# Transposing the decayed keys of a gated linear attention with VectorE and DMA in place of TensorE, with the state product one group later

## Chip, cores and metric

The kernel runs on one core of a Trainium2 chip, as one launch. The metric is the device time of that launch in microseconds (us); lower is better. All data are float32. A product that needs full precision is made of three matmuls of split operands (high x high, low x high, high x low).

## What is computed

The reference is one layer of a hybrid encoder, for 2048 positions of width 1024. One projection of x feeds two groups of heads: group A, a gated linear attention that runs over the positions in both directions, and group B, a latent attention with softmax. Their outputs go through one output projection, then a residual and a layer norm. The change lies in the backward direction of group A. Cut to that, for each head (dk 64, dv 128):

```
q_dec  = qc * exp(b)            # b: running sum of the log decay in a chunk
k_dec  = kc * exp(-b)
k_tail = kc * exp(b_last - b)
attn   = where(mask, q_dec . k_dec, 0)
o_intra = attn . vc
# from chunk to chunk:
o     = q_dec . state
state = state * exp(b_last) + k_tail^T . vc
```

The kernel works in 16 chunks of 128 positions.

## The kernel before, in words

**Stages.** `sweep_a` (L625) takes the chunks from 15 down to 0, one step for each. Then come `late_gates` (L1095), which trace the gate products of chunks 15 and 14 and load the weights of group B, and `sweep_c` (L1119), which runs over the chunks upwards. Attention and the output projection follow.

**A step of the first sweep** (step i, chunk c = 15 - i) has four groups of TensorE products over eight slices of the width: `products` with g = 0, 1, 2 (tile `ipa`, L425 to L427) and, as group 3, `gate_products` (tile `ipg`, L885), each with eight times three matmuls. Group 0 gives q and the low-rank decay input lr, group 1 gives k and a part of v, group 2 the rest of v, group 3 the gate. What hangs on them for this chunk and the chunk before is put between the matmuls. These pieces are:

- `lrT` (L929): transpose of lr on TensorE, then `z` (the log decay) and its running sums with scans on VectorE, E1 = exp(b), E2 = exp(-b) on ScalarE;
- `qx`, `kx` (L821, L834): q and k are turned by a VectorE transpose in 32x32 blocks, written with four DMAs to DRAM (`qx_s`, `kx_s`) so that the blocks land in their transposed places, and read back by `turned` (L829) with two loads each;
- `q`, `k` (L991, L1005): the decayed `qd` and `kd`, with the key dimension on the partitions;
- `kt` (L1018): four TensorE transposes of `kd`, one per head, so that the positions stand on the partitions, evicted to SBUF by ScalarE (`hi`, L371);
- `intra` (L1029): the products `Ap`, copied and masked into `At`;
- `av` (L1043): `Op` = At . V, evicted by ScalarE to `oi` and stored to DRAM (`oi_s`);
- `state` (L1054): `Up` = kt^T . V, scaled on VectorE into `Us` and stored (`su_s`); GpSimd forms `Sm` and the running state `Sb` (L1072 to L1091).

**What sets the order.** For the steps 4 to 15 the table `STEPS_A` names what follows matmul k of group g, as `(g, k)`; "prev" is the chunk of the step before, "cur" the chunk of the step. `in_order` (L387) then pins the order of the traced instructions on every engine. Steps 0 to 3 follow a list written out by hand (`ORDER_A`). What follows step 15 in the sweep (the last chunk's `q`, `k`, gate products, `kt`, `intra`, `state`, `av`) is traced in L760 to L772. What stands after the sweep and isn't pinned, such as the `memset` that clears the forward state `Sf` (L1138) or the weight splits of `late_gates` (`wmh` on ScalarE, `wml` on VectorE, both L371/L377), is placed by the scheduler that builds the program.

**Queues.** Nearly all DMAs of the sweep are issued on SyncE (SP) and its queue is in order; for chunks 1 and 0 the stores go on GpSimd's queue (`store`, L921). SP also issues the loads of x: `xaf` for the steps' own products, `xbf` (at L491) for the late gates in step 15, `xcf` for `sweep_c`, and the weights `wmr`, `wzr`.

**Buffers.** The tiles of the sweep that hold one chunk (`t512`, L926) come from the pool `g1`, most with a single buffer; its space is used by `sweep_c`'s tiles later.

Of the kernel before, what the change touches and what calls it, by code (L numbers as in the profile page):

```python
# [9 lines left out]
F32 = mybir.dt.float32  # L10
# [8 lines left out]
P = 128  # L19
# [3 lines left out]
NCH = S // P  # L23
H = 4
# [33 lines left out]
av.2 av.2 gs.3 cw.3 gs.3  # L58
"""

STEPS_A = {(0, 3): [("k", "prev")], (1, 2): [("ld", "next")], (1, 4): [("kt", "prev"), ("lrT", "cur")],
           (1, 7): [("z", "cur", 5), ("intra", "prev"), ("z", "cur", 4)], (2, 3): [("state", "prev")],
           (2, 7): [("z", "cur"), ("cw", "cur")], (3, 2): [("q", "cur")], (3, 3): [("av", "prev")]}
STEPS_A_FIRST = {**STEPS_A, (0, 3): [("q", "prev"), ("k", "prev")]}
STEPS_A_LAST = {**STEPS_A, (1, 2): [], (1, 6): [("z", "cur", 5)], (1, 7): [("intra", "prev"), ("z", "cur", 4)]}
ENGINES = tuple(getattr(mybir.EngineType, n) for n in ("PE", "Activation", "DVE", "Pool", "SP"))
LATE_ORDER = ENGINES[1], ENGINES[3], ENGINES[4]
# [293 lines left out]
class K:  # L361
# [145 lines left out]
    def run(self):  # L507
        tc, nc, ins = self.tc, self.nc, self.ins
        with ExitStack() as top:
            cp = top.enter_context(tc.tile_pool(name="const", bufs=1))  # L510
            self.cp = cp
            dp = top.enter_context(tc.tile_pool(name="scr", bufs=1, space=DRAM))
            self.qd_s = [dp.tile([P, H * P], F32, name=f"qd_s{c}") for c in range(NCH)]
            self.oi_s = [dp.tile([P, H * P], F32, name=f"oi_s{c}") for c in range(NCH)]
            self.su_s = [dp.tile([P, H * P], F32, name=f"su_s{c}") for c in range(NCH)]
            self.u_s = [dp.tile([P, H * P], F32, name=f"u_s{c}") for c in range(NCH)]
            self.qa_s = [[dp.tile([P, H, QB], F32, name=f"q{p}_s{b}") for p in "hl"] for b in range(NQB)]
            self.qr_s = [[dp.tile([H, 64, QB], F32, name=f"r{p}_s{b}") for p in "hl"] for b in range(NQB)]
            self.gm_s = [dp.tile([P, H, QB], F32, name=f"gm_s{b}") for b in range(NQB)]
            self.oa_s = [dp.tile([P, H, P], F32, name=f"oa_s{c}") for c in range(NCH)]  # L520
            self.qk_s = [[dp.tile([64, H, P], F32, name=f"{n}_s{c}") for c in range(NCH)] for n in ("qx", "kx")]
            self.r_s = [dp.tile([1, H, QB], F32, name=f"r_s{b}") for b in range(NQB)]
            self.ob_s = [dp.tile([P, H, QB], F32, name=f"ob_s{b}") for b in range(NQB)]

            ident = cp.tile([P, P], F32, name="ident")
            self.ident = ident
            self.gkv_c = cp.tile([P, 1], F32, name="gkv_c")
            self.gn_c = cp.tile([P, 1], F32, name="gn_c")
            self.cw = cp.tile([P, NCH, 3, H], F32, name="cw")

            psum = ExitStack()
            pspool = lambda n: psum.enter_context(tc.tile_pool(name=n, bufs=2, space=PSUM, reuse_waits="tile"))
            self.gp, self.ip, self.tr = pspool("gp"), pspool("ip"), pspool("tr")
            self.xfp = top.enter_context(tc.tile_pool(name="xfp", bufs=2, reuse_waits="tile"))
            edge = top.enter_context(tc.tile_pool(name="edge", bufs=1, side="right"))
            edge.tile([P, 8], F32, name="edge")
            self.keep = top.enter_context(tc.tile_pool(name="keep", bufs=1, side="right", reuse_waits="tile"))
            wgs = ExitStack()
            self.wgp = wgs.enter_context(tc.tile_pool(name="wgp", bufs=2 * NK + 1, side="right", reuse_waits="tile"))
            self.xab = wgs.enter_context(tc.tile_pool(name="xab", bufs=2, side="right"))  # L540
            self.wgate = []
            self.wl = None
            self.sweep_a()
            self.wz = top.enter_context(tc.tile_pool(name="wz", bufs=2 * NK + 1, reuse_waits="tile"))
            bcs = ExitStack()
            self.wm = bcs.enter_context(tc.tile_pool(name="wm", bufs=2 * NK + 1, reuse_waits="tile"))
            self.bc = bcs.enter_context(tc.tile_pool(name="bc", bufs=1, reuse_waits="tile"))
            self.wl = bcs.enter_context(tc.tile_pool(name="wl", bufs=2, reuse_waits="tile"))
            self.late_gates()
            wgs.close()  # L550
            rp = top.enter_context(tc.tile_pool(name="res", bufs=1, side="right", reuse_waits="tile"))
            self.ckvT_h = rp.tile([P, NKT, P], F32R, name="ckvT_h")
            self.ckvT_l = rp.tile([P, NKT, P], F32R, name="ckvT_l")
            self.kr = rp.tile([P, NKT, P], F32R, name="krs")
            self.vh = rp.tile([P, NKT, P], F32R, name="vh")
            self.vl = rp.tile([P, NKT, P], F32R, name="vl")
            self.sweep_c()
            bcs.close()
            psum.close()
            self.wof = top.enter_context(tc.tile_pool(name="wof", bufs=PRE_W, side="right", reuse_waits="tile"))  # L560
            self.attention()
# [63 lines left out]
    def sweep_a(self):  # L625
        tc, nc, ins, cp = self.tc, self.nc, self.ins, self.cp
        with ExitStack() as ctx:
# [21 lines left out]
            with tc.tile_pool(name="sta", bufs=1, reuse_waits="tile") as sta:  # L649
# [5 lines left out]
                for g, (_, n) in enumerate(A_GROUPS):  # L655
                    k = 0
# [28 lines left out]
            g1 = ctx.enter_context(tc.tile_pool(name="g1", bufs=1))  # L685
# [5 lines left out]
            run = lambda n, i: [0 for _ in getattr(self, "ga_" + n)(ch[i])]  # L691
# [9 lines left out]
            def step(i, steps):  # L701

                def after(g, k):
                    for n, d, *count in steps.get((g, k), ()):
                        j = {"prev": i - 1, "cur": i, "next": i + 2}[d]
                        if n == "ld":
                            if j < NCH:
                                next(self.ga_ld(j))
                        elif count:
                            some(n, j, *count)  # L710
                        elif (n, j) in begun:
                            for _ in begun.pop((n, j)):
                                pass
                        else:
                            run(n, j)
                for g in range(3):
                    for k in self.products(ch[i], g, after):
                        pass
                    after(g, NK - 1)
                if i and ch[i]["c"] not in LATE_GATES:  # L720
                    for k in self.gate_products(ch[i]["c"], *ch[i]["x"], ip):
                        after(3, k)
                    self.gate_end(ch[i]["c"], g1)

            self.first_lr = wdone[7][0]
            step(0, {(1, 5): [("lrT", "cur")]})
            ch[1]["x"] = self.split_x(xp, xnext, NCH - 2, "xa", "dve", 2)
            run("bst", 0)
            self.wgr = [self.wgp.tile([P, 512], F32, tag="wg", name=f"wgr{k}") for k in range(NK)]
            for k, raw in enumerate(self.wgr):  # L730
# [3 lines left out]
            for t in ORDER_A.split():  # L734
                n, i = t.split(".")
# [7 lines left out]
            for i in range(4, NCH):  # L743
                c = ch[i]["c"]
                with self.in_order(last):
# [3 lines left out]
                    else:  # L749
                        self.xlate = [self.split_x(xp, self.xb, NCH - 1, "xb")]  # L750
                        self.xraw = self.load_x(NCH - 2, "xb")
                    step(i, STEPS_A_FIRST if i == 4 else STEPS_A if c else STEPS_A_LAST)
                    if c == 1:
# [3 lines left out]
                if i == 12:  # L757
                    assert next(rope, None) is None
                    self.rope_tables(hpi)
            i = NCH - 1  # L760
            run("q", i)
            run("k", i)
            run("av", i - 1)
            for k in self.gate_products(0, *ch[i]["x"], ip):
                if k == 5:
                    run("kt", i)
            self.xlate.append(self.split_x(self.xab, self.xraw, NCH - 2, "xb", "dve", 2))
# [237 lines left out]
    def ga_k(self, d):  # L1005

        nc, c = self.nc, d["c"]
        kT = d.get("kT")
        if kT is None:
            kT = d["tr"].tile([P, H, P], F32, tag="tr", name=f"kT{c}")  # L1010
            for h in range(H):
                nc.tensor.transpose(kT[:, h], d["k2"][:, h].rearrange("p a d -> p (a d)"), self.ident)
            yield
        kd = d["kd"] = self.t512(d, "kd")
        nc.vector.tensor_tensor(kd, kT, d["E2"], ALU.mult)
        yield

    def ga_kt(self, d):  # L1018
# [1044 lines left out]
```

## Time and profile before

| | |
|---|---|
| median of three runs | 1285.17 us (1284.21 to 1286.22) |
| profiled execution | 1286.1 us, of which the span is 1284.3 us |
| TensorE (PE) busy | 1259.7 us, 98% |
| VectorE (DVE) busy | 899.4 us, 70% |
| ScalarE (ACT) busy | 755.5 us, 59% |
| GpSimd (POOL) busy | 761.1 us, 59% |
| granted TensorE clock, mean | 0.998 |
| DMA moved | 155.25 MB, mean 121 GB/s |

A row of a timeline reads: start and duration in us, engine, line of the kernel, operation, out<-in by the program's names, shape, and count of like instructions that are drawn together; in brackets, the idle time of the engine just before and what ended it. PEld is TensorE's weight load, SPq the queue of DMA issues on SyncE. In the table of waits each row is an engine's instruction, what it waited for, the total, the count and the longest in us. The steady part of the first sweep lies between 80 and 310 us; the step of chunk 0 begins at 316.76 us.

### The profile page before, as it was taken

What the parts mean: (1) busy time and instruction counts of PE and PEld (TensorE: products, weight loads), DVE (VectorE), ACT (ScalarE), POOL (GpSimd) and SP (SyncE); (2) the same over time, 40 slices, a digit from 0 to 9 for tenths busy, and PEclk for the clock granted to TensorE, in tenths of its full rate; (3) what the DMA queues carried; (4) which work ended last, traced back from release to release, by engine and by line L of the source; (5) the groups of instructions that cost most, each with busy time, mean ns of one, the idle gap of its engine ahead of it and who ended that gap; (6) DMA issues with size and microseconds to landing.
All of it is one profiled execution on the core that took longest, in us unless ns stands there. A gap on an engine that the chain in (4) does not pass through costs nothing.

```text
span 1284.3 us, 19837 instructions
## 1 busy us (share of the span) xinstructions
PE 1259.7 (98%) x7050; PEld 1109.9 (86%) x7050; DVE 899.4 (70%) x1602; ACT 755.5 (59%) x1230; POOL 761.1 (59%) x476
## 2 busy tenths in 40 slices
PE   7999999999999999999999999999999999999997
PEld 7999999999889999999788888888888888887886
DVE  6635554544575555554888888888888888479997
ACT  7544343444565655555788888888888888511110
POOL 0132323222367666650498888889999999944541
PEclk9999999999999999999999999999999999999999
DMA  8223444444755666547201111111133110375752
GB/s 293 78 79 108 115 111 114 115 105 126 255 171 184 205 205 210 194 149 228 76 1 42 41 42 50 46 54 58 58 89 93 41 42 9 123 227 193 220 189 99
DMA packets 135746, 155.25 MB, mean 121 GB/s; under 512 B 43510, under 2 KB 86142, under 8 KB 135648
## 3 DMA queue, kind: packets, MB, share of 16 engines
q1 hardware_dynamic: 127584, 151.86, 38.4%
q0 software_dynamic: 672, 2.10, 0.4%
q8 instruction: 56, 0.92, 0.4%
q10 hardware_dynamic: 7392, 0.03, 0.3%
q14 instruction: 42, 0.34, 0.2%
HBM read 100.43 MB, written 53.51 MB: 120 GB/s over the span
## 4 chain that ended last, share of the span: by engine, by line
PE 82%; DMA 5%; DVE 4%; ACT 2%; issue 2%; POOL 2%; SPq 2%; DVEq 0%; POOLq 0%; ACTq 0%
PE pz L1237 6%; PE ipm L1308 5%; PE o L425 4%; PE o L426 4%; PE o L427 4%; PE pS L1569 4%; PE pS L1570 4%; PE pS L1572 4%; PE pS L1571 4%; PE pS L1573 4%; PE ipa L425 4%; PE ipa L427 4%; PE ipa L426 4%; PE ipg L427 2%; PE ipg L425 2%
## 5 line engine op out<-in xcount | busy, mean ns | idle before, releaser
L377 POOL TENSOR_TENSOR pl<-s,ph 128x1024 fp32r<-128x1024 f32 x128 | 306.4, 2411 | 57.7 <-ACT ph L371 53.8
L1591 DVE TENSOR_TENSOR rm<-pS,rm 128x512 f32<-128x512 f32 x210 | 144.8, 689 | 36.7 <-ACT s L1578 31.5
L1578 ACT ACTIVATE s<-pS 128x1024 f32<-128x1024 f32 x128 | 131.2, 1026 | 61.8 <-PE pS L1573 52.0
L1615 DVE TENSOR_TENSOR s<-s,mb 128x1024 f32<-128x1024 f32 x128 | 151.2, 1212 | 8.9 <-PE mb L1609 8.2
L371 ACT ACTIVATE ph<-s 128x1024 fp32r<-128x1024 f32 x128 | 135.1, 1057 | 16.9 <-PE o L427 16.4
L1619 ACT ACTIVATE s<-s 128x1024 f32<-128x1024 f32 x128 | 131.4, 1050 | 12.2 <-DVE s L1615 12.1
L425 PE MATMUL ipa<-wah,xah 128*128 128x384 f32 (+1 forms) x384 | 129.7, 338 | 5.5 <-ACT wah L371 5.5
L426 PE MATMUL ipa<-wal,xah 128*128 128x384 f32 (+1 forms) x384 | 124.5, 324 | 0.5 <-DVE wal L377 0.5
L427 PE MATMUL ipa<-wah,xal 128*128 128x384 f32 (+1 forms) x384 | 124.4, 324 | 0.0
L1569 PE MATMUL pS<-qh,ckvT_h 128*128 128x512 f32 x256 | 102.7, 401 | 2.0 <-ACT s L1578 1.2
L1072 POOL TENSOR_TENSOR Sb<-Sb,Us 64x512 f32<-64x512 f32 x15 | 20.9, 1394 | 136.9 <-DVE Us L1064 127.8
L425 PE MATMUL o<-ph,vh 128*128 128x512 f32 x256 | 101.0, 395 | 0.0
L1570 PE MATMUL pS<-ql,ckvT_h 128*128 128x512 f32 x256 | 100.0, 391 | 0.0
L1572 PE MATMUL pS<-rh,krs 128*128 128x512 f32 x256 | 99.9, 390 | 0.0
L1571 PE MATMUL pS<-qh,ckvT_l 128*128 128x512 f32 x256 | 99.9, 390 | 0.0
L1573 PE MATMUL pS<-rl,krs 128*128 128x512 f32 x256 | 99.8, 390 | 0.0
L427 PE MATMUL o<-ph,vl 128*128 128x512 f32 x256 | 99.7, 389 | 0.0
L426 PE MATMUL o<-pl,vh 128*128 128x512 f32 x256 | 99.6, 389 | 0.0
L1642 DVE TENSOR_TENSOR ap<-ap,s 128x512 f32<-128x512 f32 x120 | 83.1, 693 | 2.7 <-ACT s L1619 0.7
L377 POOL TENSOR_TENSOR xal<-xaf,xah 128x1024 fp32r<-128x1024 f32 x12 | 29.7, 2477 | 87.8 <-ACT xah L371 87.8
L377 POOL TENSOR_TENSOR ol<-of,oh 128x512 fp32r<-128x512 f32 x32 | 43.2, 1352 | 62.6 <-ACT oh L371 61.9
L425 PEld LDWEIGHTS ipa<-wah,xah 128*128 128x128 f32 x384 | 72.9, 190 | 7.8 <-ACT wah L371 5.5
(308 smaller groups left out, 3595.6 us busy)
## 6 DMA issues: line engine op xcount, KB each, us to landing
xcf<-xT_dram SPq DMA_DIRECT2D x16, 512.0 KB, 5.1
xr<-x_dram SPq DMA_DIRECT2D x16, 512.0 KB, 6.4
out_dram<-rr SPq DMA_DIRECT2D x32, 256.0 KB, 2.2
xaf<-xT_dram SPq DMA_DIRECT2D x14, 512.0 KB, 4.2
oib<-oi_s SPq DMA_DIRECT2D x16, 256.0 KB, 4.0
qdb<-qd_s SPq DMA_DIRECT2D x16, 256.0 KB, 4.0
SU<-su_s SPq DMA_DIRECT2D x16, 256.0 KB, 4.1
ub<-u_s SPq DMA_DIRECT2D x16, 256.0 KB, 4.2
```

The costliest lines, as they stand in the source:

```text
L371: return nc.scalar.activation(dst, src, AF.Copy).ins
L377: return e.tensor_tensor(dst, src, hi.bitcast(F32), ALU.subtract).ins
L425: mm(out, ah, bh, start=start, stop=False)
L426: mm(out, ah, bl, start=False, stop=False)
L427: mm(out, al, bh, start=False, stop=stop)
L1569: mm(ps[:, e], kh, qh, start=True, stop=False)
L1570: mm(ps[:, e], kh, ql, start=False, stop=False)
L1571: mm(ps[:, e], kl, qh, start=False, stop=False)
L1572: mm(ps[:, e], kr, rh, start=False, stop=False)
L1573: mm(ps[:, e], kr, rl, start=False, stop=True)
L1591: V.tensor_tensor(d["rm"], src[:, e], d["rm"], ALU.max)
L1615: V.tensor_tensor(s, s, d["mb"][:, None, :].to_broadcast([P, 2, QB]), ALU.subtract)
```

## The change

For the chunks of i = 4 to 14 `kt` on TensorE is replaced by two pieces:

- `kx2`: VectorE transposes `kd` in 32x32 blocks (128 x 512), and four DMAs on SP write the result to a new DRAM tensor `kt_s`, 64 KB each, in pieces of 32 elements;
- `ktl`: one DMA of 256 KB on SP reads `kt` back into SBUF.

`kx2` stands at (1, 4), where `kt` stood, behind `lrT`; `ktl` at (2, 4). `state`, which consumes `kt`, moves from (2, 3) to (3, 6), that is ahead of the last three matmuls of the gate. Step 4, which handles chunk i = 3, keeps the old places. The chunk i = 15 still uses TensorE; the state of chunk i = 14 is traced after the third group of three matmuls of the last gate product (k == 2).

In the order of instructions: TensorE has 44 transposes fewer (11 x 4), ScalarE 11 evictions fewer, VectorE 11 transposes more, SP 55 DMA issues more. On SP the stores `su_s` of `Us` and `Sm` now stand behind the loads of k and the store of `oi`; in the last step `xbf` still stands behind them. TensorE's late-gate matmuls of `xb` stand in part ahead of the last chunk's `kt`, `Ap`, `Up` and `Op` (24 of 48, where 3 stood). On VectorE the `memset` of `Sf` stands ahead of all eight `wml`, where it stood behind five. From the first `wm` weights on the rest of the order is the same. Line numbers in the changed kernel are 2 higher from L64 on, 3 from L521, 5 from L764 and 19 from L1016 on.

```diff
--- before.py
+++ after.py
@@ -58,10 +58,12 @@
 av.2 av.2 gs.3 cw.3 gs.3
 """
 
-STEPS_A = {(0, 3): [("k", "prev")], (1, 2): [("ld", "next")], (1, 4): [("kt", "prev"), ("lrT", "cur")],
-           (1, 7): [("z", "cur", 5), ("intra", "prev"), ("z", "cur", 4)], (2, 3): [("state", "prev")],
-           (2, 7): [("z", "cur"), ("cw", "cur")], (3, 2): [("q", "cur")], (3, 3): [("av", "prev")]}
-STEPS_A_FIRST = {**STEPS_A, (0, 3): [("q", "prev"), ("k", "prev")]}
+STEPS_A = {(0, 3): [("k", "prev")], (1, 2): [("ld", "next")], (1, 4): [("lrT", "cur"), ("kx2", "prev")],
+           (1, 7): [("z", "cur", 5), ("intra", "prev"), ("z", "cur", 4)], (2, 4): [("ktl", "prev")],
+           (2, 7): [("z", "cur"), ("cw", "cur")], (3, 2): [("q", "cur")], (3, 3): [("av", "prev")],
+           (3, 6): [("state", "prev")]}
+STEPS_A_FIRST = {**STEPS_A, (0, 3): [("q", "prev"), ("k", "prev")], (1, 4): [("kt", "prev"), ("lrT", "cur")],
+                 (2, 3): [("state", "prev")], (2, 4): [], (3, 6): []}
 STEPS_A_LAST = {**STEPS_A, (1, 2): [], (1, 6): [("z", "cur", 5)], (1, 7): [("intra", "prev"), ("z", "cur", 4)]}
 ENGINES = tuple(getattr(mybir.EngineType, n) for n in ("PE", "Activation", "DVE", "Pool", "SP"))
 LATE_ORDER = ENGINES[1], ENGINES[3], ENGINES[4]
@@ -519,6 +521,7 @@
             self.gm_s = [dp.tile([P, H, QB], F32, name=f"gm_s{b}") for b in range(NQB)]
             self.oa_s = [dp.tile([P, H, P], F32, name=f"oa_s{c}") for c in range(NCH)]
             self.qk_s = [[dp.tile([64, H, P], F32, name=f"{n}_s{c}") for c in range(NCH)] for n in ("qx", "kx")]
+            self.kt_s = [dp.tile([P, H, P], F32, name=f"kt_s{c}") for c in range(NCH)]
             self.r_s = [dp.tile([1, H, QB], F32, name=f"r_s{b}") for b in range(NQB)]
             self.ob_s = [dp.tile([P, H, QB], F32, name=f"ob_s{b}") for b in range(NQB)]
 
@@ -762,6 +765,8 @@
             run("k", i)
             run("av", i - 1)
             for k in self.gate_products(0, *ch[i]["x"], ip):
+                if k == 2:
+                    run("state", i - 1)
                 if k == 5:
                     run("kt", i)
             self.xlate.append(self.split_x(self.xab, self.xraw, NCH - 2, "xb", "dve", 2))
@@ -1013,6 +1018,20 @@
             yield
         kd = d["kd"] = self.t512(d, "kd")
         nc.vector.tensor_tensor(kd, kT, d["E2"], ALU.mult)
+        yield
+
+    def ga_kx2(self, d):
+
+        t = d["g1"].tile([P, H, 4, 32], F32, tag="ktx", name=f"ktx_{d['c']}")
+        self.nc.vector.transpose(t.rearrange("p h a s -> p (h a s)"), d["kd"].rearrange("p h s -> p (h s)"))
+        dst = self.kt_s[d["c"]].rearrange("(a r) h (b t) -> b r h a t", a=4, b=4)
+        for b in range(4):
+            self.nc.sync.dma_start(dst[b], t[32 * b:32 * b + 32])
+        yield
+
+    def ga_ktl(self, d):
+        d["kt"] = self.t512(d, "kt")
+        self.nc.sync.dma_start(d["kt"], self.kt_s[d["c"]])
         yield
 
     def ga_kt(self, d):
```

## Prediction

> **What bounds the kernel now.** I read the busy table first, then busy time by stretch, then PE's waits, and last the timelines of the engines at the places where PE waits.
>
> ```profile
> span 1284.3 us, 19837 instructions
> PE 1259.7 (98%) x7050; PEld 1109.9 (86%) x7050; DVE 899.4 (70%) x1602; ACT 755.5 (59%) x1230; POOL 761.1 (59%) x476
> ```
> ```profile
> 80.00:310.00 230.00, 228.87 (x1497) 215.51 (x1496) 114.83 (x207) 100.14 (x201) 64.69 (x43) 1.00 0.41 109
> 380.00:620.00 240.00, 237.54 (x1669) 225.65 (x1668) 129.80 (x440) 140.13 (x357) 140.09 (x144) 1.00 0.59 194
> ```
> ```profile
> PE kt L1023 <- DVE kd L1015: 1.6, 1, 1.6
> PE ipm L1308 <- DVE xcl L377: 1.2, 1, 1.2
> PE lrT L933 <- DVE lr L377: 1.1, 1, 1.1
> PE Op L1047 <- DVE At L1040: 0.6, 1, 0.6
> ```
>
> The columns of the stretches are us, then PE, PEld, DVE, ACT and POOL busy. In the steady part of the first sweep (80 to 310 us) PE is busy 228.87 of 230 us, and the only wait of PE there is the 1.1 us of lrT. DVE (114.83) and ACT (100.14) are half idle. So in that stretch the kernel is bound by PE, and PE work taken out comes off the time, unless a later place cannot use it. The other three waits listed lie between 338 and 357 us, where the sweep hands over to the next stage. After 380 us PE is full again (237.54 of 240), so whatever the handover yields, plus or minus, stays to the end.
>
> **What the change removes.** Eleven chunks (4 to 14) lose four PE transposes and one ACT eviction each.
>
> ```profile
> 194.34 0.34 PE L427 MATMUL ipa<-wah,xal 128*128 128x384 f32 x1
> 194.52 0.60 PE L1023 MATMUL kt<-ident,kd 128*128 128x128 f32 x4
> 194.95 0.27 PE L933 MATMUL lrT<-ident,lr 128*98 128x128 f32 x1
> 194.98 0.42 PE L425 MATMUL ipa<-wah,xah 128*128 128x384 f32 x1
> ```
> ```profile
> L1023 PE MATMUL kt<-ident,kd x44: 270/272/273, 88.9 to 301.8; 128*128 128x128 f32 x44
> L371 ACT ACTIVATE kt<-kt x11: 597/597/599, 89.6 to 302.1; 128x512 f32<-128x512 f32 x11
> ```
>
> One transpose lasts 272 ns, but they are pipelined: what PE gives up is the spacing of starts. From the first kt (194.52) to lrT (194.95) are 0.43 us for four; I take 0.44, so 11 x 0.44 = 4.8 us at most. The eviction, 0.597 us, is on an engine with over half its time free, so I count nothing for it.
>
> One of the eleven gives nothing by itself. The 1.1 us wait of lrT in the list stands right behind a kt: PE waits there for lr, and without kt it comes 0.44 earlier and waits 0.44 longer. The chunk whose transposes stand in the last step is treated below. So up to the start of the last step 9 x 0.44 = **3.96 us** are saved.
>
> **What the change adds in each step.** A DVE transpose of 128x512, four stores to DRAM and one load, all on SP's queue; the state product Up moves from the third group of products to just before the last three gate matmuls (of 24) of the step. I lay this out in the step that begins at 188.74 and is followed by the next at 209.86 (21.12 us).
>
> ```profile
> 188.74 0.29 PE L425 MATMUL ipa<-wah,xah 128*128 128x288 f32 x1
> ...
> 209.63 0.39 PE L427 MATMUL ipg<-wgh,xal 128*128 128x512 f32 x1
> 209.86 0.29 PE L425 MATMUL ipa<-wah,xah 128*128 128x288 f32 x1
> ```
> ```profile
> 196.85 0.45 DVE L824 STREAM_TRANSPOSE kx<-ipa 128x256 f32<-128x256 f32 x1 [3.81 <-PE ipa L427]
> ```
> ```profile
> 193.07 2.59 SPq L827 DMA_DIRECT2D qx_s<-qx  x4
> 195.70 0.60 SPq L491 DMA_DIRECT2D xaf<-xT_dram  x1
> 197.09 1.62 SPq L832 DMA_DIRECT2D q<-qx_s  x2
> 198.82 2.82 SPq L827 DMA_DIRECT2D kx_s<-kx  x4
> ```
> ```profile
> DMA to landing us min/median/max: 2.2/3.0/3.4
> ```
> ```profile
> oib<-oi_s SPq DMA_DIRECT2D x16, 256.0 KB, 4.0
> ```
>
> DVE: the transpose of 128x256 takes 0.45, so twice the width lies between 0.45 and 0.9; I take 0.85. DVE idles 3.81 us just after this place (the bracket of the row), which hides it; without that cover it would delay kx, which feeds only the next step. SP: qx_s and xaf end at 196.30. The four kt_s come next. A qx_s issue takes 2.59 / 4 = 0.65 for 64 partitions' worth of half as many pieces as a kt_s; nothing in the trace issues 512 pieces of 128 bytes, so a kt_s lies between 0.65 (the cost is per issue) and 1.3 (per piece). I take 0.65, because a row of the same kind of store is nearest, and keep the other end as a rival. Then kt_s runs to 198.9 and lands by 198.9 + 3.4 = 202.3 (the landing line is that of kx_s); q to 200.5, kx_s to 203.35, the load of kt issues at 203.4 and lands 4.0 later (the 256 KB row), at **207.4**. Up starts 0.44 + 3 x 0.23 + 0.92 before 209.86, at **207.8** (0.23 is the spacing of the last two rows of PE above, 0.92 that of Up below). It is in time by 0.4 us, so each step costs nothing more. SP has 3.0 us more work in a step of 21 and keeps room.
>
> **The last step.** Here one transfer is moved past something. SP's queue is in order. Before, it issues the store of Us and of Sm of the step before at 312.21 and 312.75, and the load xbf at 316.45, 0.31 ahead of the step's start (316.76). ACT splits xbf before it evicts lr, and lrT waits for lr.
>
> ```profile
> 312.21 0.49 SPq L1065 DMA_DIRECT2D su_s<-Us  x1
> ...
> 316.45 0.83 SPq L491 DMA_DIRECT2D xbf<-xT_dram  x2
> ```
> ```profile
> 321.02 1.06 ACT L371 ACTIVATE xbh<-xbf 128x1024 fp32r<-128x1024 f32 x1 [2.13 <-DMA xbf<-xT_dram]
> ```
> ```profile
> 316.76 0.29 PE L425 MATMUL ipa<-wah,xah 128*128 128x288 f32 x1
> ```
> ```profile
> 322.55 0.60 PE L1023 MATMUL kt<-ident,kd 128*128 128x128 f32 x4
> 322.98 0.27 PE L933 MATMUL lrT<-ident,lr 128*98 128x128 f32 x1
> ...
> 338.32 0.66 PE L1023 MATMUL kt<-ident,kd 128*128 128x128 f32 x4 [1.64 <-DVE kd L1015]
> ...
> 341.39 1.16 PE L1061 MATMUL Up<-V,kt 128*128 128x128 f32 x8
> 343.82 1.16 PE L1047 MATMUL Op<-V,At 128*128 128x128 f32 x8 [0.57 <-DVE At L1040]
> ```
>
> In the changed order Up ends 3 x 0.23 = 0.7 before the step's start (call it T); Us needs about 0.8 more, so the two su_s issue (0.49 and 0.5) until T + 1.2, and xbf, behind them, at about **T + 1.4** instead of T - 0.31. It lands 4.48 after its issue now (316.45 to 320.94, 0.08 before xbh starts) and lrT is ready 1.6 after that landing (xbh 1.06, two small ACT copies, the small DVE one). That gives T + 7.45. PE is there at 322.55 - 316.76 = T + 5.79, with no kt ahead of lrT any more. So PE gets a new wait of 1.66; lrT stands at T + 7.45 instead of T + 6.22, **1.23 later**. The 0.44 of the eleventh kt is in that.
>
> Further on in the last step the changed order puts 24 of the two late gates' 48 matmuls (ipg from xb) ahead of the last Op, where 3 stood: 21 x 0.23 = **4.8 later**. In exchange kt's 1.64 wait for kd is covered (Us and kd now run beside 13 of these matmuls). The 0.57 before Op stays, as no matmul is left between Up and Op. Sum for the last Op, and for oi, its eviction and its store: -3.96 + 1.23 + 4.8 - 1.64 = **+0.4**: the stores end no earlier, while PE has 21 matmuls fewer to fill the time after it.
>
> **The handover.** DVE clears Sf, whose place in SBUF is that of the sweep's tiles, and so waits for the landing of the last oi store.
>
> ```profile
> 346.11 3.49 DVE L377 TENSOR_TENSOR wml<-wmr,wmh 128x448 fp32r<-128x448 f32 x5 [1.18 <-ACT wmh L371]
> 352.53 0.48 DVE L1138 MEMSET Sf<- 64x512 f32 x1 [2.93 <-DMA oi_s<-oi]
> 352.94 2.65 DVE L377 TENSOR_TENSOR wml<-wmr,wmh 128x448 fp32r<-128x448 f32 x3
> 355.50 2.35 DVE L377 TENSOR_TENSOR xcl<-xcf,xch 128x1024 fp32r<-128x1024 f32 x2
> ```
> ```profile
> 345.90 0.57 POOL L1051 DMA_DIRECT2D oi_s<-oi  x1
> ```
> ```profile
> 356.77 0.47 PE L1308 MATMUL ipm<-wmh,xcl 128*128 128x448 f32 x1 [1.16 <-DVE xcl L377]
> ```
>
> Now five of the eight wml subtractions stand ahead of the memset, three and xcl behind it, and PE's third ipm matmul waits 1.16 for xcl: DVE is already last here. In the changed program's order on DVE the memset stands ahead of **all eight**. The five that used to fill the wait (3.49 us by the row) now queue behind it, ahead of xcl. With oi's landing 0.4 later, xcl is ready 3.5 + 0.4 = **3.9 us later**, and PE cannot use what it saved: it waits at ipm for some 9 us instead of 1.16. DVE then runs without a pause into the weights of the next product, so nothing is given back before PE is full again from 380 us on.
>
> So a gain of 3.96 us is eaten at the handover, and 3.9 us are lost on top. The profiled execution took 1286.1 us (0.9 above the median of 1285.17) and would become 1290.0; against the median, 1285.2 + 3.9 = **1289.1**.
>
> **The rivals.**
>
> *Faster: the handover does not bind.* If the memset's wait, or DVE's order, is not what ends last at ipm, PE keeps its 4.8 less the 0.44 of the step with the lr wait: 1285.2 - 4.4 = 1280.8. For it speaks that PE is the busy engine on both sides. Against it: to let PE through, xcl would have to start near 350, nine us before the 359 that this order gives, so the memset would have to run at 343.6, before the last oi store is issued (345.90). It decides only if the Sf wait disappears.
>
> *xbf is not late.* If xbf lands in 2.8 instead of 4.48 (kx_s lands in 2.2 to 3.4 in the row above), the new 1.66 wait at lrT vanishes and only 3.9 - 1.7 = 2.2 are lost: 1287.4. For: SP's queue and the DMA engines have some other load at that moment. Against: the two xbf loads are 512 KB each.
>
> *The last oi store lands sooner.* It takes 352.53 - 345.90 = 6.6 now, beside the sixteen weight loads; at 3.4 the memset comes 3.2 earlier and 0.7 remain: 1285.9. The weight loads are issued some 2 us earlier than before in the new queue, which speaks for part of it.
>
> *kt is late at Up in every step.* With kt_s at more than 0.75 an issue the 0.4 of slack is gone; at 0.85 (0.8 more over four) Up waits 0.4 in each of ten steps, and 4.0 come on top: 1293.1; at the far end of 1.3 it would be 2.2 in each step, past 1310. Against it: the rows of the smaller stores show no cost that grows with the pieces. The Trainium skill, "DMA: Bandwidth & Descriptors", section "Specifications", speaks for it: transfers below 512 bytes fall short of the line rate, since the DMA engine then does a read-modify-write. By that rule kt_s, in pieces of 128 bytes, would be slow in landing, not only in issue; the landings of kx_s, with the same pieces, show 2.2 to 3.4 us, and no run here shows a kt_s.
>
> That the change does not do what it says isn't possible in substance: the changed program's order shows the transposes gone from PE.
>
> **How the numbers follow.** Forecast 1289.1: 0.44. xbf in time, 1287.4: 0.16. Earlier landing of oi, 1285.9: 0.12. kt late, 1293.1: 0.16. Faster, 1280.8: 0.12. A measurement of this kernel can tell about 0.2% (2.6 us) from no change: 1282.6 to 1287.7 is "the same". That holds the second and third case: 0.28; faster 0.12; slower 0.44 + 0.16 = 0.60. The range 1285.0 to 1293.4 holds all but the faster case and the far end of the late kt.
>
> **What would show it.** (1) No kt on PE between the fifth and the last step, steps 0.43 shorter, the last step's start near 312.8. (2) PE's waits: none on Up behind a DMA (else kt is late). (3) A wait of about 1.7 at lrT in the last step, released by ACT or DVE lr, and xbf issued 1.4 after the step's start. (4) The last Op near 344.2 as now. (5) DVE: memset of Sf at about 352.9 with its wait on oi_s, eight wml behind it, xcl at about 359, and a wait of some 9 us at ipm for it. If (5) shows the memset before 349, or ipm's wait under 5 us, the forecast is wrong, and the time goes to the side of the faster case.

## The result, and the profile after

The changed kernel takes 1290.34 us (median of five runs, 1290.03 to 1292.13) against 1285.3 before: ratio 1.0042, interval 1.0028 to 1.0057, so 5.0 us slower. The forecast was 1289.1. The profiled execution of the changed kernel took 1292.13, the slowest of its five; it is 6.0 above the profiled execution of before (1286.1), and its trace is read against that.

The waits of PE from 80 to 420 us, after:

```profile
PE ipm L1327 <- DVE xcl L379: 7.4, 1, 7.4
PE lrT L938 <- DVE lr L379: 2.7, 2, 1.6
PE ipm L1327 <- DVE wml L379: 2.0, 1, 2.0
PE ipg L427 <- DVE Us L1083: 1.1, 1, 1.1
PE Up L1080 <- DMA kt<-kt_s: 1.0, 1, 1.0
PE Op L1066 <- DVE At L1059: 0.4, 1, 0.4
```

The list answers to the one shown of before. Its 1.6 of kt and 1.2 of ipm are gone; ipm now waits twice, 7.4 + 2.0 = 9.4 us at one place. Next the timelines there: PE's last Op and the first matmuls of ipm, DVE, and the GpSimd queue.

```profile
344.39 1.16 PE L1066 MATMUL Op<-V,At 128*128 128x128 f32 x8 [0.37 <-DVE At L1059]
...
352.26 0.36 PE L1327 MATMUL ipm<-wmh,xch 128*128 128x448 f32 x1
354.61 0.47 PE L1327 MATMUL ipm<-wml,xch 128*128 128x448 f32 x1 [1.99 <-DVE wml L379]
362.49 0.74 PE L1327 MATMUL ipm<-wmh,xcl 128*128 128x448 f32 x1 [7.41 <-DVE xcl L379]
```
```profile
345.93 0.69 DVE L1083 TENSOR_TENSOR Us<-Up,cw 128x512 f32<-128x512 f32 x1 [1.02 <-DMA su_s<-Us]
353.59 0.48 DVE L1157 MEMSET Sf<- 64x512 f32 x1 [6.97 <-DMA oi_s<-oi]
354.00 6.23 DVE L379 TENSOR_TENSOR wml<-wmr,wmh 128x448 fp32r<-128x448 f32 x8
360.15 4.26 DVE L379 TENSOR_TENSOR xcl<-xcf,xch 128x1024 fp32r<-128x1024 f32 x2
```
```profile
346.92 0.55 POOL L1084 DMA_DIRECT2D su_s<-Us  x1 [1.15 <-DVE Us L1083]
347.45 0.57 POOL L1070 DMA_DIRECT2D oi_s<-oi  x1
359.61 1.74 POOL L1456 TENSOR_TENSOR Sf<-Sf,SU 64x512 f32<-64x512 f32 x1 [4.16 <-DMA SU<-su_s]
361.43 1.90 POOL L1461 TENSOR_TENSOR SU<-Sf,cw 64x512 f32<-64x512 f32 x1
```

DVE stands idle for 6.97 us before the memset, while ScalarE makes the high parts that the wml need (wmh, all eight done by 349.9), and then does all eight wml and xcl in a row. Three ipm matmuls in, PE is 362.49 - 356.77 = 5.7 us behind the kernel before. Then something comes that the prediction had not: the stretches of 4 us around it (behind the length of 4.00 stands PE's busy time; the last but two is the granted clock).

```profile
352.00:356.00 4.00, 1.09 (x4) 0.38 (x3) 2.25 (x3) 3.97 (x8) 1.28 (x1) 0.87 0.83 238
356.00:360.00 4.00, 0.00 (x0) 0.00 (x0) 3.52 (x6) 3.94 (x8) 0.39 (x1) 0.50 0.77 242
360.00:364.00 4.00, 1.51 (x4) 1.38 (x5) 4.00 (x3) 0.74 (x3) 3.25 (x2) 0.50 0.01 3
364.00:368.00 4.00, 4.00 (x12) 3.52 (x12) 3.69 (x6) 0.99 (x3) 0.00 (x0) 0.50 0.53 168
368.00:372.00 4.00, 4.00 (x29) 3.84 (x28) 3.68 (x9) 0.00 (x0) 0.00 (x0) 0.93 0.34 94
```

The wait has taken PE's clock down to 0.50, and it stays there until 368. In 364 to 368 PE is busy all the time and gets through 12 matmuls; in the four us behind it, 29.

How far the lag reaches is read from two tiles, first and last start of pz and pS (the attention's first product), before and after:

```profile
L1237 PE MATMUL pz<-xch,wzh x256: 278/283/375, 363.0 to 593.7; 128*128 128x256 f32 x128
```
```profile
L1569 PE MATMUL pS<-qh,ckvT_h x256: 389/389/497, 597.7 to 1077.4; 128*128 128x512 f32 x128
```
```profile
L1256 PE MATMUL pz<-xch,wzh x256: 277/283/389, 371.5 to 601.2; 128*128 128x256 f32 x128
```
```profile
L1588 PE MATMUL pS<-qh,ckvT_h x256: 389/389/478, 605.2 to 1083.4; 128*128 128x512 f32 x128
```

The lag is 8.5 us at the first pz (5.7 plus 2.8 of the slow clock), 7.5 at the last, and 6.0 at the last pS. So 2.5 of it are given back. Of these, 1.2 are a single wait of PE at pS for ScalarE that the execution of before has and this one hasn't.

In the steady part the change does what it is for. lrT, once in each step, starts 21.12 us apart before; after, two of them stand at

```profile
192.68 0.27 PE L938 MATMUL lrT<-ident,lr 128*98 128x128 f32 x1
...
213.32 0.27 PE L938 MATMUL lrT<-ident,lr 128*98 128x128 f32 x1
```

which is 20.64: 0.48 saved in each undisturbed step. The last step begins at 313.80 instead of 316.76, and 2.96 are in hand there.

### The profile page after: what moved, and what is told of

It is laid out like the page before. It is cut to its first block, busy times and chain, and to the rows that moved or that the text cites. A ratio compares the mean times of both kernels' runs of the same rounds, so it can differ in the third digit from the quotient of the medians.

```text
span 1290.4 us, 19839 instructions
## 1 busy us (share of the span) xinstructions
PE 1258.3 (98%) x7006; PEld 1107.4 (86%) x7006; DVE 896.5 (69%) x1613; ACT 750.4 (58%) x1219; POOL 761.2 (59%) x476
## 4 chain that ended last, share of the span: by engine, by line
PE 65%; DVE 3%; issue 1%; DMA 1%; ACT 1%; POOL 0%; DVEq 0%; SPq 0%; POOLq 0%
PE pz L1256 7%; PE ipm L1327 6%; PE o L427 4%; PE o L428 4%; PE o L429 4%; PE pS L1588 4%; PE pS L1589 4%; PE pS L1591 4%; PE pS L1590 4%; PE pS L1592 4%; PE po L429 2%; PE po L427 2%; PE po L428 2%; PE Ob L1484 1%; PE pmb L427 1%
## 5 line engine op out<-in xcount | busy, mean ns | idle before, releaser
L428 PEld LDWEIGHTS ipa<-wal,xah 128*128 128x128 f32 x384 | 73.0, 190 | 1.4 <-DVE wal L379 0.9
```

The lines of the kernel that those rows point to most:

```text
L428: mm(out, ah, bl, start=False, stop=False)
```

## The experiments

Times are medians; the ratio is to the kernel before measured beside each (1285.0 to 1285.4), with its 95% interval. "Late memset" is the edit of the first. Code is cut to the lines that matter, with "..." where lines are left out; the cuts of 6 and 7 are written against the kernel before. Traces are of single executions, and their sweeps don't start at the same moment: the first lrT lies between 67.83 and 69.53 us (68.52 before the change, 68.56 after).

**1. The memset of Sf behind xcl, in the changed kernel.**

```diff
...
-            self.nc.vector.memset(Sf, 0.0)
+            clear = self.nc.vector.memset(Sf, 0.0).ins
+            self.tc.add_manual_dep(clear, self.xcl_tail[1].name, mybir.DependencyInfo(
+                mybir.DependencyClass.NoSync, mybir.DependencyReason.DATA), reason="in_order")
```

> The changed kernel with one edit: the memset of Sf is put behind the second xcl subtraction on DVE, so that no wml or xcl stands behind its wait for the last oi store. Theory (the loss sits at the handover): the eight wml run from about 346.7 to 352.9, the first xcl ends near 354.2, PE's third ipm matmul starts near 354.3 instead of 362.5, and PE's clock no longer drops. 2.4 us ahead of the kernel before at that place: 1282.8, some 7.5 below the changed kernel. Rival (the 55 DMAs and the moved state cost the time in the sweep itself): at most 2 us come back, 1288 or more.

1283.07, ratio 0.9987 (0.9978 to 0.9996). PE and DVE there:

```profile
353.42 0.47 PE L1330 MATMUL ipm<-wmh,xcl 128*128 128x448 f32 x1 [1.35 <-DVE xcl L379]
```
```profile
346.59 5.64 DVE L379 TENSOR_TENSOR wml<-wmr,wmh 128x448 fp32r<-128x448 f32 x8 [0.73 <-ACT wmh L373]
352.14 1.22 DVE L379 TENSOR_TENSOR xcl<-xcf,xch 128x1024 fp32r<-128x1024 f32 x1
```

(`xcl_tail[1]` is the second xcl subtraction; the dependency fixes the order on DVE and nothing else.) One reordered instruction brings 7.3 us back; ipm's third matmul starts 9.1 earlier.

**2. The same edit in the kernel before.**

> The kernel before with the same edit alone: the memset of Sf behind the second xcl. Theory: PE's 1.16 wait at ipm goes, 1284.1 (1.2 below before); it is the right base for the edited change. Rival (DVE's order at the handover does not end last in the kernel before): 1285.3, unchanged.

1284.0, ratio 0.9993 (0.9984 to 1.0001). The trace shows the third ipm matmul without a wait; in the time, the 1.0 us to the kernel before beside it (1285.0) can't quite be told from none. With both on a late memset, the change is worth 0.9 us, and the intervals overlap.

**3. The wait alone, in the kernel before.** The late memset, and a memset of the last oi tile on DVE, which must wait for the landing of the same store, ahead of the first wml:

```diff
...
             run("av", i)
+            self.oi_clear = nc.vector.memset(self.oi_last[:64], 0.0).ins
...
+        self.tc.add_manual_dep(self.parts[ENGINES[2], "wm"][0], self.oi_clear.name, mybir.DependencyInfo(
+            mybir.DependencyClass.NoSync, mybir.DependencyReason.DATA), reason="in_order")
```

> The kernel before (PE makes kt, nothing added, state in its place) with the late memset of Sf, and with a memset of 64 partitions of the last oi tile on DVE ahead of the first wml: it needs the landing of the last oi store, as Sf's memset does, so all eight wml and xcl stand behind that landing as in the changed kernel. It tells whether this one wait, with no other part of the change, makes the loss. Theory: the clear runs near 352.5, the third ipm matmul near 360 to 361 instead of 355.3, PE idles some 5 us there; with what the dropped clock costs, 1284.0 + 5 to 6 = 1289.5. Rival (the loss of the changed kernel is its own DMAs and moved state): 1284 to 1286.

1289.54, ratio 1.0031 (1.0020 to 1.0043).

```profile
352.95 0.48 DVE L773 MEMSET oi<- 64x512 f32 x1 [7.48 <-DMA oi_s<-oi]
353.36 5.57 DVE L377 TENSOR_TENSOR wml<-wmr,wmh 128x448 fp32r<-128x448 f32 x8
358.85 2.35 DVE L377 TENSOR_TENSOR xcl<-xcf,xch 128x1024 fp32r<-128x1024 f32 x2
```
```profile
360.12 0.73 PE L1314 MATMUL ipm<-wmh,xcl 128*128 128x448 f32 x1 [3.97 <-DVE xcl L377]
```

So the kernel before, with nothing of the change in it but this order, loses 5.5 us against experiment 2 and 4.2 against the kernel before. The changed kernel lost 5.0 against that, and the two intervals overlap. That the place makes the loss is shown from both sides.

**4. What the dropped clock costs.** Extra work for PE while it would wait, in the changed kernel:

```diff
...
+            warm = self.tr.tile([P, H, P], F32, tag="tr", name="warm")
+            for k in range(80):
+                nc.tensor.transpose(warm[:, k % H], self.ident, self.ident)
...
```

> The changed kernel with 80 extra 128x128 transposes of the identity on PE between the late gates and the first ipm matmul, into a PSUM tile that nobody reads; PE is then busy while it would wait for DVE. It tells what the dropped clock (0.50 from 356 to 368 us) costs apart from the wait. Theory: the clock stays at 1.0, ipm's 24 matmuls of the first chunk run at 0.2 instead of 0.37 apart, pz starts 2.8 earlier, total 1287.5. Rival (DVE's wzl set the pace behind ipm anyway, or the clock drop is only a record): 1290.3, unchanged or slower by what the extra work overshoots.

1288.5, ratio 1.0027 (1.0016 to 1.0037): 1.8 below the changed kernel, with intervals that overlap. The stretch that had a clock of 0.50:

```profile
360.00:364.00 4.00, 3.39 (x17) 3.16 (x18) 3.91 (x5) 1.63 (x4) 1.45 (x1) 1.00 0.01 4
```

The clock stays at 1.00. The wait is still there, hidden under useless work; the slow matmuls behind it are not. From the third ipm matmul to the first pz are 6.3 us here, 9.0 in the changed kernel and 6.2 in the kernel before. (That matmul itself starts 1.9 earlier here, at 360.61, because the memset came at 351.70; the extra work has no part in that.)

**5. The most that can be gained.** The kernel before, late memset, with the transposes of kd left out for the eleven chunks:

```diff
...
+    def ga_kn(self, d):
+        d["kt"] = d["kd"]
...
```

> The kernel before with the late memset, and without the transposes of kd and their evictions for chunks i = 4 to 14: the state product reads kd in place of kt (so its values are not the reference's), nothing is added and state stays where it was. It is the most that the change can gain. Theory: 11 x 0.44 less one that falls in a wait, so 4.4 below the late-memset kernel before, 1279.7. Rival (the handover eats it, as DVE, the loads or the wait for kd end last there): less than 2 below it.

1278.57, ratio 0.9954 (0.9941 to 0.9966): 5.4 below experiment 2; the 4.4 that were expected lie within the intervals.

**6. The additions alone.** The DVE transpose and the five DMAs beside a kt that PE still makes:

```diff
-(1, 4): [("kt", "prev"), ("lrT", "cur")],
+(1, 4): [("kt", "prev"), ("lrT", "cur"), ("kx2", "prev")], (2, 4): [("ktl", "prev")],
```

> The additions alone: ktx turned by DVE, four kt_s stores and a 256 KB load for chunks i = 4 to 13 (into a tile that nobody reads), while PE and ACT still make kt and state stays where it was; late memset; the last step issues none of them. Theory: they lie beside PE's work, the last step starts where it does in the kernel before (316.6 to 316.8): 1284.0, up to 1 above it for the scheduler's other order at the tail. Rival (pieces of 128 bytes in the DMA engines and SP's queue hold up loads that the sweep waits for): the last step starts 1 us or more later, 1285.5 or more.

1286.27, ratio 1.0009 (1.0000 to 1.0018), 2.3 above experiment 2: the rival's number, with runs from 1284.28 to 1289.93. The trace splits it. The steady steps cost nothing: lrT starts at 195.71 and 216.83, 21.12 apart as before. The whole sweep lies 0.9 later than in experiment 2, from the first lrT on (69.27 against 68.35). The loss begins in the last step, where SP has the load of kt ahead of xbf:

```profile
314.14 0.58 SPq L1031 DMA_DIRECT2D kt<-kt_s  x1
314.90 1.87 SPq L835 DMA_DIRECT2D k<-kx_s  x2
317.44 1.17 SPq L493 DMA_DIRECT2D xbf<-xT_dram  x2
```

lrT waits 1.2 us there, a wait that experiment 2 doesn't have at that place. The queue is the smaller part of it: xbf is issued 0.08 ahead of the step's start (317.52), against 0.33 in experiment 2, but it lands 6.0 after its issue instead of 4.8. Whether the loads ahead of it make that longer landing is not shown, since experiment 3, with none of the additions, has 5.7. So the pieces of 128 bytes cost nothing in the steady steps; in the last step the rival isn't excluded. The scheduler's order of the last late-gate matmuls differs too (eight ahead of the last Op, not three), and how the 2.3 divide is open.

**7. The moved state alone,** kt on PE, late memset:

```diff
-           ... (2, 3): [("state", "prev")],
+           ... (3, 6): [("state", "prev")]
```

> The change's second half alone: state moved to just before the last three gate matmuls, kt still by PE and ACT for all chunks, late memset. Theory: nothing is saved; in the last step xbf stands behind the later su_s and lrT waits longer, and four more late-gate matmuls stand ahead of the last Op: 1.5 to 2.5 above the late-memset kernel before (1284.0), 1286.0. Rival (moving state is free): 1284.0.

1285.43, ratio 1.0001 (0.9992 to 1.0010), 1.4 above experiment 2, with intervals that overlap. lrT of the last step waits 1.1, with xbf issued 1.8 after the step's start (317.15):

```profile
318.33 0.59 SPq L1107 DMA_DIRECT2D su_s<-Sm  x1
318.97 1.07 SPq L493 DMA_DIRECT2D xbf<-xT_dram  x2
```

Here it is the place in the queue that makes xbf late: it lands 4.1 after its issue. Eight late-gate matmuls stand ahead of the last Op here too.

**8. xbf ahead,** in the changed kernel with the late memset:

```diff
-                    if c == 1:
-                        self.xb = self.load_x(NCH - 1, "xb")
...
+step(i, {**STEPS_A, (2, 2): [("xb", "cur")]} if c == 1 else STEPS_A if c else STEPS_A_LAST)
```

> The changed kernel with the late memset and the first xbf load issued in the step before, ahead of the load of kt. The scheduler then also puts 18 late-gate matmuls ahead of the last Op instead of 24. Theory (the wait of lrT in the last step was xbf's, and the last Op sets the handover): the 1.1 us wait at lrT in the last step goes, the last Op comes 1.1 and a further 6 x 0.23 earlier, at about 341.8, and the total is 1.3 below the late-memset changed kernel (1283.1), its wait for xcl being gone: 1281.4. Rival (PE's wait only moves to another place): 1283.1.

1280.71, ratio 0.9964 (0.9951 to 0.9976), 2.4 below experiment 1; 1281.4 was expected. lrT's wait in the last step is gone, the last Op starts at 341.94. Six late-gate matmuls fewer stand ahead of that Op (18, not 24), and what each of the two is worth isn't separated.

**9. The last step as before,** with 1 and 8:

```diff
-STEPS_A_LAST = {**STEPS_A, (1, 2): [],
+STEPS_A_LAST = {**STEPS_A, (1, 4): [("kt", "prev"), ("lrT", "cur")], (2, 3): [("state", "prev")], (2, 4): [], (3, 6): [], (1, 2): [],
...
-                if k == 2:
-                    run("state", i - 1)
```

> The changed kernel with three edits: the late memset of Sf; the first xbf load issued in the step before, ahead of the load of kt; and the last step as in the kernel before (kt of chunk i = 14 on PE, its state in the third group, so ten chunks are turned by DVE and DMA instead of eleven, and PE's order at the end of the sweep is that of the late-memset kernel before). Theory (the steady steps do save 0.44 each, and only the last step and the handover give it back): 9 x 0.44 = 4.0 below the late-memset kernel before (1284.0), 1280.0, with the last Op at 339.7 and no wait of PE above 1 us but lrT's in step 13 and kt's. Rival (the additions cost about what the transposes save): 1283 or more, and the last step would begin later than 313.2.

1281.9, ratio 0.9974 (0.9964 to 0.9984): between theory (1280.0) and rival (1283), somewhat nearer the rival. The last step begins at 313.42, past the rival's 313.2, and the last Op stands at 340.44; PE still waits 1.0 at Up for kt in one step, which the theory had left out.

**10. kt's stores early,** in the changed kernel with the memset in its bad place:

```diff
-... (1, 4): [("lrT", "cur"), ("kx2", "prev")], ... (2, 4): [("ktl", "prev")],
+... (0, 5): [("kx2", "prev")], ... (1, 4): [("lrT", "cur")], ... (2, 1): [("ktl", "prev")],
...
```

> The changed kernel with the DVE transpose and its four kt_s stores moved to right behind kd (group 0, matmul 5) and the load of kt to group 2, matmul 1; the memset of Sf stays ahead of the wml. It tells whether kt's late landing at Up (0.98 in the step behind the long wait for lr) costs time. Theory: that wait goes, the last step begins 1.0 earlier, the last Op and with it the chain to the memset come 1.0 earlier: 1289.3 against 1290.3. Rival (the wait is made up elsewhere): 1290.3; other rival (ktx ahead of lr on DVE delays lrT in each step): above 1291.

1290.04, ratio 1.0036 (1.0023 to 1.0049), against 1.0042 for the changed kernel: the times can't be told apart. The list of PE's waits has no Up any more, and the last Op starts at 342.62 instead of 344.39. So early stores take that wait away; what it is worth at the end is open.

**11. Two buffers for Us,** on top of 8:

```diff
-        Us = self.t512(d, "Us")
+        Us = self.t512(d, "Us", bufs=2)
```

> The changed kernel with the late memset, the early xbf and two buffers for Us (the changed kernel has one, and its last Us waits 1.0 to 1.3 for the landing of the store of the one before; the oi store on GpSimd's queue stands behind the store of Us). Theory: that wait and the half microsecond at ipm go, 0.7 below the same without the second buffer (1280.7): 1280.0. Rival (DVE's wzl set the pace next): 1280.7.

1280.4, ratio 0.9966 (0.9953 to 0.9978). DVE's wait of Us for the store is gone in the trace; the time can't be told from experiment 8.

**12. Everything together** (1, 8, 10, 11):

> The same with the early transpose and stores of kt as well: everything that was found to give time back is taken away. Theory: kt is never late (1.6 in two places), so 1279.0, close to the kernel that leaves the transposes out (1278.6). Rival (the landing of kt is not what is late, or lr is delayed by ktx ahead of it on DVE): 1280.5 or more.

1281.4, ratio 0.9963 (0.9950 to 0.9975), the rival's side of its bound, with runs from 1279.07 to 1281.93. No Up wait is left, but PE now waits 1.6 for xcl and 2.6 for a weight load:

```profile
PE pabs L1223 <- DMA wqT<-wqT_dram: 2.6, 1, 2.6
PE ipm L1330 <- DVE xcl L379: 1.6, 1, 1.6
```

8, 11 and 12 have the lowest times of the kernels that keep the whole computation, about 0.35% below the kernel before, and can't be told from each other; the interval of 9 overlaps with theirs. What PE gains beyond them goes into the next wait of the handover.

## Why the prediction was right, by its own steps

- **What PE saves in a step.** Right in kind, the size was 0.44 and is 0.48: the step is 20.64 instead of 21.12. Experiment 5 shows the same saving without the DMAs (192.67 to 213.32). Where the other 0.04 of a step lie wasn't traced.
- **The step with the long wait for lr saves nothing.** Right: its lrT waits 1.57 instead of 1.13.
- **kt is in time at Up.** Right in nine steps of ten, wrong in one, where PE waits 0.98. It follows the step's long wait at lrT: lr is late, so qx and ktx behind it on DVE are late. On top of that one issue of qx_s takes 1.68, so that the four take 3.66 instead of 2.58. SP issues kt_s at 281.70 and the load at 288.47.

```profile
277.30 3.66 SPq L832 DMA_DIRECT2D qx_s<-qx  x4
281.00 0.61 SPq L493 DMA_DIRECT2D xaf<-xT_dram  x1
281.70 2.59 SPq L1029 DMA_DIRECT2D kt_s<-ktx  x4
...
288.47 0.54 SPq L1034 DMA_DIRECT2D kt<-kt_s  x1
```
```profile
291.46 0.80 PE L1080 MATMUL Up<-V,kt 128*128 128x128 f32 x5 [0.98 <-DMA kt<-kt_s]
```

  This is the rival of the late kt, in one place. Its price per issue didn't come true: four kt_s take 2.59, or 0.65 each, as assumed. What ate the slack of 0.4 was a late start, and its size goes with the qx_s: in the six traces with kt_s at this place, PE's wait in this step is 0, 0.51, 0.56, 0.90, 0.98 and 1.00 us where the four qx_s take 2.74, 3.21, 3.33, 3.63, 3.66 and 3.67 (experiments 1, 4, 11, 8, the changed kernel, 9). Why that issue is long is open. With the stores early (experiments 10 and 12) the wait is gone. The DMAs of kt_s, stores and loads together, landed in 2.2 to 5.5, median 3.6; those of kx_s in the kernel before in 2.0 to 5.0, median 2.7. Eight steps save 3.8 together, but this one is 0.8 longer than before, so 2.96 are in hand ahead of the last step, not 3.96.
- **xbf is late in the last step.** Right: issued 1.43 after the step's start (315.23 against 313.80; 1.4 was forecast). It landed in 4.0 instead of 4.48, so lrT's wait is 1.11 instead of 1.66 and lrT stands 0.83 later in the step, not 1.23. In experiment 8, with xbf early, this wait is gone.
- **The last Op.** +0.4 was forecast, +0.57 measured (343.82 to 344.39). That this is so near is luck in part. The terms were -3.96, +1.23 and 4.8 - 1.64 = +3.16; they came out at -2.96, +0.83 and +2.70. The saving was 1.0 too large and the two others together 0.9 too large, which nearly cancelled.
- **The memset ahead of all eight wml.** Right, and the cause of the loss: experiments 1 and 3 take it away and put it in alone. Its size was 3.9 at the third ipm matmul and is 5.7. Two things were missed. Us has one buffer, so the last Us waits 1.02 for a store, and the store of oi stands behind that of Us on GpSimd's queue: it is issued at 347.45 instead of 345.90 and the memset comes at 353.59, 1.06 later, where 0.4 was forecast. And the two xcl take 4.26 instead of 2.35, beside GpSimd's work on Sf, by which the first, for which PE waits, ends 1.1 later. Eight wml instead of three behind the memset make 3.6, where 3.5 was forecast: 1.06 + 3.6 + 1.1 = 5.7.
- **The end.** 3.9 was forecast, 5.0 is the time. The forecast had PE's clock at nothing and said that nothing is given back. In the profiled execution the clock adds 2.8 to the 5.7 at ipm, and 2.5 are gone again by the last pS (8.5 to 6.0). The two omissions nearly cancel, so that the number came so near is luck in part; the place, the wait and its cause are not.

The rivals: "faster" needed the Sf wait to vanish, and experiment 1 is that case: it gives 1283.1, not 1280.8. DVE still ends last there: PE waits 1.35 for xcl at ipm and 1.1 for wzl at pz. "xbf in time" didn't happen. "The last oi store lands sooner" came true by 0.5 us only: from issue to memset 6.1, against 6.6, not 3.4.

## What to carry to other kernels

A change that frees the busiest engine is worth what the next handover lets through: follow the saved time to the first place where another engine ends last, and compare the order of instructions there, also of those that the change doesn't touch. An instruction that needs a late landing (here a clearing memset whose space a store still reads) must stand behind all work of its engine that doesn't need it; pin it, if a scheduler chooses. When a producer is moved later, look at what stands behind its store in an in-order queue.

## What the runs showed of the hardware

- **PE's clock falls in a wait of some us and is slow to come back.** After 9.4 us of waiting the granted clock is 0.50, and sixteen matmuls of ipm run 0.37 us apart instead of 0.20, until 368.6, 6.1 us after PE has work again. In experiment 3 a wait of 4.0 did it too:

```profile
360.00:364.00 4.00, 3.88 (x11) 3.49 (x12) 3.86 (x6) 1.62 (x3) 1.50 (x2) 0.57 0.30 88
364.00:368.00 4.00, 4.00 (x29) 3.78 (x28) 3.73 (x4) 1.01 (x3) 2.84 (x2) 1.00 0.54 178
```

  In stretches of half a microsecond the clock is back 3.5 us after PE has work there, and 3.1 in experiment 10, behind a wait of 8.2. So the price differs from execution to execution: from the third ipm matmul to the first pz are 9.0 us in the changed kernel, 7.9 in experiment 3 and 7.7 in experiment 10, against 6.2 at full clock, which is 2.8, 1.7 and 1.5. A wait of 2.60 in experiment 12 (353.82 + 0.37 to 356.79) left the clock at 1.00:

```profile
352.00:356.00 4.00, 2.19 (x11) 1.69 (x9) 3.64 (x5) 3.94 (x8) 1.35 (x1) 1.00 0.89 196
356.00:360.00 4.00, 3.21 (x28) 3.24 (x29) 3.73 (x5) 0.06 (x1) 2.42 (x2) 1.00 0.97 358
```

  The Trainium skill, "TensorE: Matmul & The Clock Gate", section "Why this matters for your kernels", says to leave no gap of more than about 3 us between bursts of matmuls, or the clock falls to half. Experiments 3 and 12 agree, on both sides of that bound. After the change the records put the fall at about 354.95, behind a gap of 1.99 and one matmul and ahead of the long wait (355.08), so there a shorter gap was enough.
- **DVE's subtraction of two SBUF tensors slows beside GpSimd.** The first xcl takes 1.22 in experiment 1, and the two take 4.26 after the change, while GpSimd's Sf and SU stand at 1.74 and 1.90 instead of 1.29 and 1.37. In experiment 3, where GpSimd has nothing to do until 362.43, the two xcl take 2.35 in the same order. Its eight wzl, beside GpSimd's Sf, take 8.35, and those of the changed kernel, with GpSimd idle, 6.16:

```profile
362.26 8.35 DVE L377 TENSOR_TENSOR wzl<-wzr,wzh 128x512 fp32r<-128x512 f32 x8
```
```profile
364.94 6.16 DVE L379 TENSOR_TENSOR wzl<-wzr,wzh 128x512 fp32r<-128x512 f32 x8
```

  The Trainium skill, "SBUF — State Buffer", section "SBUF: two separate sides", has the two engines share a port pair that one instruction holds to its end. The durations fit that; the port itself is in no trace here.
